# A feed-forward block split in two stages: seven half-size products for gate and up, with the gated values kept in DRAM

## The chip, the cores and the metric

The kernel runs on one core of a Trainium2 chip. The metric is the device time in microseconds of one execution. The core has a matrix engine (PE, with a weight-load side called PEld), a vector engine (DVE), a scalar engine (ACT), GpSimd (POOL) and a sync engine (SP) whose queue issues most DMAs. The profile gives times from the start of its span.

## The reference, cut to what matters

One layer: a mixing block (an RG-LRU next to RWKV-7 heads), its output projection, a gated feed-forward network, a gated embedding, and a last norm. There are S = 512 tokens, D = 2048 features and D_FF = 6144. The change touches the feed-forward part:

```
h = h + concat(out_a, out_b) @ w_o
u = rmsnorm(h, ln_ffn)
gate = causal_dwconv(u @ w_gate, conv_f_w, conv_f_b)      # 3 taps over tokens
h = h + (gelu(gate) * (u @ w_up)) @ w_down
u = rmsnorm(h, ln_ple)                                    # then the gated embedding
```

All is float32. Every matrix product is made of three: each operand is split into a high part hi (rounded to fp32r) and the rest lo, and hi x hi, hi x lo and lo x hi are added in PSUM.

## The kernel before, in words

Values are held with features on partitions: a tile hT[m] is 128 features by 512 tokens. `wqueue` gets the list of all weight tiles in the order of use. `wfill` (L105) keeps two of them ahead of the product that is at work: it loads a raw tile of 128x1024 (SP queue, two buffers), ACT copies it to hi (L127), DVE subtracts to get lo (L128); hi and lo have three buffers each. An entry of the list can be a function that makes the raw tile itself (loads, sums). `wfill` runs with a raised priority. In this phase no order is written out by hand: instructions go to the queues of the engines by priority, which is the order of the program with such offsets, and each queue is worked off in order.

`phase2` begins with the second part of the output projection (16 row tiles; L1188 adds to hT, L143/L144 split it as the operand u of the next products, POOL sums squares).

The FFN runs in one interleaved order, `ffn_order`. For each of 48 feature tiles f of D_FF and for gate and up there are two units of 8 k-tiles: 24 matmuls of 128x128 weights against 512 tokens (L1216 to L1218). L1238 to L1244 scale the gate by the token norm, apply the convolution and the gelu, and multiply by the norm once more (POOL); L1249 multiplies by up. Four tiles f make a chunk of 512 hidden features, kept in SBUF; `hidden` forms its operands.

The down product of a chunk uses a seven-product scheme (Winograd's form of Strassen's method) on halves of hidden features, tokens and output columns: 7 products of half size for 8. `down_unit` makes the sums of weight blocks; one block is added to another in SBUF by a DMA from the POOL queue that accumulates (L1127). Each product has 12 matmuls of 512 columns (L1298 to L1300), and DVE adds it out of PSUM to the running sums (L1313). The 14 down units of a chunk are spread between the gate/up units of the next. The last chunk is done plainly (`down_last`), followed for each block of 512 output columns by `to_features` (transposes and splits for the next stage). The residual hT is transposed to tokens-on-partitions early, in `turn`, during the first chunk.

After that come the gated embedding (L1389 to L1391; the last quarter is 256 columns wide) and the final norm.

Of the kernel before, what the change touches and what calls it, by code (L numbers as in the profile page):

```python
# [4 lines left out]
F32 = mybir.dt.float32  # L5
# [6 lines left out]
D = 2048  # L12
# [9 lines left out]
FC = 4  # L22
C = 64
# [62 lines left out]
class Builder:  # L86
# [149 lines left out]
    def xsplit(self, k):  # L236
        return (self.t(self.bp, "xh%d" % k, (128, S), F32R, bufs=1),
                self.t(self.bp, "xl%d" % k, (128, S), F32R, bufs=1))
# [827 lines left out]
    def wo_a(self, m):  # L1066
        nc, A, k1 = self.nc, self.A, self.k1
        if m == 0:
            self.out_a(range(4, 8))
            self.hT = [self.bp.tile([128, S], F32, tag="x%s%d" % ("hl"[i // 8], 8 + i % 8), name="hT%d" % i, bufs=1)  # L1070
                       for i in range(KT)]
# [29 lines left out]
    def ffn_order(self):  # L1101
        g = lambda f: [("g", f, w, h) for w in range(2) for h in range(2)]
        o = sum([g(f) for f in range(FC)], [])
        nch = NF // FC
        for ch in range(nch - 1):
            q = [("q", ch, b, i) for b in range(2) for i in range(7)]
            o += g((ch + 1) * FC)
            n = sum([g((ch + 1) * FC + i) for i in range(1, FC)], [])
            k = 0
            for i, x in enumerate(q):  # L1110
                o.append(x)
                e = (i + 1) * len(n) // len(q)
                o += n[k:e]
                k = e
        o += [("d", cb, kh) for cb in range(4) for kh in range(2)]
        return o


    def down_unit(self, ch, b, i):
        nc = self.nc  # L1120

        def load(kh, nh):
            t = self.t(self.k2, "hw%d" % (2 * kh + nh), (128, 2, 512), bufs=1)
            nc.sync.dma_start(t, self.A["wd"][ch, b, kh, nh])
            return t
        def add(t, kh, nh):
            nc.gpsimd.dma_start(t, self.A["wd"][ch, b, kh, nh], accum_op=ALU.add)  # L1127

        def sum_of(kh, nh):
            t = self.t(self.k2, "hw4" if nh == 0 else "hw1", (128, 2, 512), bufs=1)  # L1130
            nc.sync.dma_start(t, self.A["wd"][ch, b, kh, nh])
            return t
        if i == 0:
            self.qt = sum_of(0, 0)
            add(self.qt, 0, 1)
            return load(0, 0)
        if i == 1:
            self.qs = sum_of(0, 1)
            add(self.qs, 1, 1)
            return self.qt  # L1140
        if i == 2:
            add(self.qt, 1, 1)
            return self.qt
        if i == 3:
            return load(1, 1)
        if i == 4:
            return self.qs
        if i == 5:
            return load(1, 0)
        add(self.qt, 1, 0)  # L1150
        return self.qt

    def ffn_items(self):
        A = self.A
        u = (128, 8, 128)
        r = []
        for o in self.ffn_order():
            if o[0] == "g":
                r.append((A["wgu"][o[1], o[2], o[3]], u))
            elif o[0] == "d":  # L1160
                r.append((A["wd"][NF // FC - 1, o[1] % 2, o[2], o[1] // 2], (128, 2, 512)))
            else:
                r.append((lambda o=o: self.down_unit(*o[1:]), (128, 2, 512)))
        for cb in range(4):
            r += [(A["wpp"][cb], (128, 2, 512))]
            if cb < 3:
                r += [(A["wpg"][cb, i], (128, 2, 512)) for i in range(8)]
        r += [(A["wpg3"][0, i], (128, 4, 256)) for i in range(2)]
        r += [(A["wpg3"][1, 0, :, 2 * i:2 * i + 2], (128, 2, 256), "hw%d" % (4 + i)) for i in range(2)]
        r += [(A["wpg3"][0, i], (128, 4, 256)) for i in range(2, 4)]  # L1170
        r += [(A["wpg3"][1, i], (128, 4, 256)) for i in range(1, 4)]
        return r


    def phase2(self):
# [8 lines left out]
        u2 = []  # L1184
        for m in range(KT):
# [3 lines left out]
            hi, lo = T("uh%d" % m, dt=F32R), T("ul%d" % m, dt=F32R)  # L1189
            self.split(hi, lo, hT[m], self.P("ln_ffn", m))  # L1190
            u2.append((hi, lo))
            if m == 0:
                SC.activation(acc, hT[m], AF.Square)
            else:
                sq = T("tmp", 2)
# [3 lines left out]
        gz = self.t(self.cp, "row", (128, S + 2), bufs=1)  # L1199
        G.memset(gz[:, 0:2], 0.0)  # L1200


        h3 = [self.bp.tile([128, S], F32, tag="x%s%d" % ("hl"[i // 8], i % 8), name="h3_%d" % i, bufs=1) for i in range(16)]

        def turn(cb):
            for tt in range(4):
                pt = self.mm()
                for i in range(4):
                    TE.transpose(pt[:, i * 128:(i + 1) * 128], hT[4 * cb + i][:, tt * 128:(tt + 1) * 128], self.K("ident"))
                SC.activation(h3[tt * 4 + cb], pt, AF.Copy)  # L1210

        def half(ps, us, h):
            wh, wl = self.wnext()
            for k in range(8):
                xh, xl = us[8 * h + k]
                TE.matmul(ps, wh[:, k, :], xh, start=h + k == 0, stop=False)  # L1216
                TE.matmul(ps, wh[:, k, :], xl, start=False, stop=False)  # L1217
                TE.matmul(ps, wl[:, k, :], xh, start=False, stop=h == 1 and k == 7)  # L1218

        raw = [None, None]  # L1220
        pgu = [None, None]
        gc = None

        def gate_up(f, which, h):
            nonlocal gc
            if h == 0:
                pgu[which] = self.aux() if f >= FC else self.mm()
            half(pgu[which], u2, h)
            if h == 0:
                return  # L1230
            if which == 0:
                if f == 0:
                    self.r2 = self.tok_rstd(acc, D, RMS_EPS, k2)
                    return
            elif f == 0:
                self.rstd_bcast(acc, D, RMS_EPS, k2, rs, self.r2)
            if which == 0 or f == 0:
                V.tensor_tensor(gz[:, 2:S + 2], pgu[0], rs, ALU.mult)  # L1238
                gc = c = T("tmp", 2)
                SC.activation(c, gz[:, 2:S + 2], AF.Identity, scale=self.P("cfw", 2 * NF + f), bias=self.P("cfb", f))  # L1240
                for w in range(2):
                    V.scalar_tensor_tensor(c, gz[:, w:w + S], self.P("cfw", w * NF + f), c, ALU.mult, ALU.add)
                SC.activation(c, c, AF.Gelu_apprx_tanh)  # L1243
                G.tensor_tensor(c, c, rs, ALU.mult)  # L1244
            if which == 1:
                i = f % FC
                if i % 2 == 0:
                    raw[i // 2] = T("hw%d" % (5 + i // 2), 1, (128, 2, 512))
                V.tensor_tensor(raw[i // 2][:, i % 2, :], gc, pgu[1], ALU.mult)  # L1249
                if i < 4:  # L1250
                    turn(i) if f < FC else None
                if i == FC - 1:
                    self.hids[f // FC] = hidden(f == NF - 1)


        a = lambda i, j: raw[j][:, :, 256 * i:256 * i + 256]

        def hidden(last):
# [335 lines left out]
```

## Time and profile before

| | us |
|---|---|
| median of 3 runs | 2648.77 (2645.67 to 2649.02) |
| the profiled execution | 2648.61 |
| its span | 2646.8 |

| stretch of the span, us | what runs there |
|---|---|
| 0 to 908 | mixing block and output projection |
| 908 to 1026 | gate and up of the first chunk |
| 1026 to 2377 | gate and up with the down products of 11 chunks |
| 2380 to 2437 | last chunk, turn to features |
| 2437 to 2647 | gated embedding, final norm |

In the page, "busy" is a sum of instruction lengths. Matmuls overlap, so that a busy PE is not yet a PE at its peak; the distance from one start to the next tells more. In a row of groups, the number after the bar is the busy time, then the mean length in ns, then the engine's idle time before these instructions and what ended it.

### The profile page before, as it was taken

Reading aid. Unit: us, or ns where it says so; the run is one execution under the profiler, and the core shown is the slowest. Engines: PE = TensorE matmul, PEld = TensorE weight load, DVE = VectorE, ACT = ScalarE, POOL = GpSimd, SP = SyncE. Lnnn points to the kernel's source line nnn. Section 1 sums busy time; section 2 is a strip of 40 time slices with the busy share of each in tenths; the row PEclk is TensorE's granted clock in tenths of the full one; section 3 lists DMA queues with packets and bytes.
Section 4 is the critical chain, followed back from the end, with each engine's and each line's share of the span. In section 5 each row is a group of like instructions: output and inputs, shape, how many; then the busy total and the mean of one; then the engine's idle time right before and its main releaser. Section 6 shows DMA issues by size and latency. Waiting matters only on the chain.

```text
span 2646.8 us, 43808 instructions
## 1 busy us (share of the span) xinstructions
PE 2602.5 (98%) x18466; PEld 2132.7 (81%) x18466; DVE 1614.5 (61%) x2332; ACT 1081.6 (41%) x1515; POOL 278.9 (11%) x265
## 2 busy tenths in 40 slices
PE   9989999999999999999999999999999999999997
PEld 8867778777877888888888888888888888888887
DVE  5764775667666535565665665666566565775447
ACT  6563555546433433333333333333333333335335
POOL 0010000101122301101011110101010111000001
PEclk9999999999999999999999999999999999999999
DMA  7222322222234324545455454545454545442223
GB/s 251 90 69 66 93 77 63 84 75 94 95 128 138 117 88 120 153 133 152 134 151 137 143 138 141 153 133 152 137 156 129 153 139 152 131 137 88 96 92 108
DMA packets 100326, 323.26 MB, mean 122 GB/s; under 512 B 11552, under 2 KB 14240, under 8 KB 100128
## 3 DMA queue, kind: packets, MB, share of 16 engines
q1 hardware_dynamic: 87456, 274.32, 30.7%
q0 software_dynamic: 12672, 46.14, 10.5%
q8 instruction: 144, 2.36, 0.4%
q14 instruction: 54, 0.44, 0.1%
HBM read 312.29 MB, written 8.13 MB: 121 GB/s over the span
## 4 chain that ended last, share of the span: by engine, by line
PE 69%; DVE 2%; DMA 1%; ACT 1%; issue 1%; POOL 0%; POOLq 0%; ACTq 0%; DVEq 0%
PE wk L1218 12%; PE wk L1217 12%; PE wk L1216 12%; PE mm L1299 6%; PE mm L1300 6%; PE mm L1298 6%; PE mm L1389 2%; PE mm L1391 2%; PE mm L1390 2%; PE mm L161 1%; PE mm L157 1%; PE mm L159 1%; PE mm L1216 1%; PE mm L1218 1%; PE mm L1217 1%
## 5 line engine op out<-in xcount | busy, mean ns | idle before, releaser
L127 ACT ACTIVATE whi<-wraw 128x1024 fp32r<-128x1024 f32 (+1 forms) x361 | 373.8, 1035 | 736.9 <-PE mm L159 194.2
L128 DVE TENSOR_TENSOR wlo<-wraw,whi 128x1024 fp32r<-128x1024 f32 (+1 forms) x361 | 441.7, 1223 | 241.5 <-ACT whi L127 235.6
L1216 PE MATMUL wk<-uh,whi 128*128 128x512 f32 x1408 | 547.9, 389 | 0.0
L1218 PE MATMUL wk<-uh,wlo 128*128 128x512 f32 x1408 | 547.8, 389 | 0.0
L1217 PE MATMUL wk<-ul,whi 128*128 128x512 f32 x1408 | 547.8, 389 | 0.0
L127 ACT ACTIVATE whi<-hw 128x1024 fp32r<-128x1024 f32 x154 | 163.4, 1061 | 488.7 <-PE wk L1217 389.9
L128 DVE TENSOR_TENSOR wlo<-hw,whi 128x1024 fp32r<-128x1024 f32 x154 | 188.7, 1226 | 243.7 <-ACT whi L127 241.3
L161 PE MATMUL mm<-xh,wlo 128*128 128x512 f32 x832 | 333.2, 400 | 1.5 <-DVE wlo L128 1.5
L157 PE MATMUL mm<-xh,whi 128*128 128x512 f32 x832 | 333.1, 400 | 1.4 <-DVE hT L447 0.9
L159 PE MATMUL mm<-xl,whi 128*128 128x512 f32 x832 | 331.8, 399 | 0.0
L1216 PEld LDWEIGHTS wk<-uh,whi 128*128 128x128 f32 x1408 | 264.3, 188 | 54.9
L1217 PEld LDWEIGHTS wk<-ul,whi 128*128 128x128 f32 x1408 | 264.3, 188 | 54.9
L1218 PEld LDWEIGHTS wk<-uh,wlo 128*128 128x128 f32 x1408 | 264.3, 188 | 54.8
L1299 PE MATMUL mm<-wlo,hid 128*128 128x512 f32 x680 | 265.2, 390 | 0.0
L1300 PE MATMUL mm<-whi,hid 128*128 128x512 f32 x680 | 264.9, 390 | 0.0
L1298 PE MATMUL mm<-whi,hid 128*128 128x512 f32 x680 | 264.9, 390 | 0.0
L157 PEld LDWEIGHTS mm<-xh,whi 128*128 128x128 f32 x832 | 157.5, 189 | 37.6 <-issue 3.0
L161 PEld LDWEIGHTS mm<-xh,wlo 128*128 128x128 f32 x832 | 157.5, 189 | 36.6 <-DVE wlo L128 2.6
L159 PEld LDWEIGHTS mm<-xl,whi 128*128 128x128 f32 x832 | 157.4, 189 | 33.7 <-issue 1.8
L1313 DVE TENSOR_TENSOR h<-h,mm 128x512 f32<-128x512 f32 x264 | 175.2, 682 | 0.9
L1244 POOL TENSOR_TENSOR tmp<-tmp,rsa 128x512 f32<-128x512 f32 x48 | 70.3, 1464 | 772.1 <-ACT tmp L1243 772.1
L1298 PEld LDWEIGHTS mm<-whi,hid 128*128 128x128 f32 x680 | 127.7, 188 | 26.4
(511 smaller groups left out, 3550.3 us busy)
## 6 DMA issues: line engine op xcount, KB each, us to landing
wraw<-wgu SPq DMA_DIRECT2D x192, 512.0 KB, 3.3
hw<-wd SPq DMA_DIRECT2D x110, 512.0 KB, 3.2
hw<-wd POOLq DMA_DIRECT2D x88, 512.0 KB, 5.5
wraw<-wz SPq DMA_DIRECT2D x80, 512.0 KB, 3.6
wraw<-wpg SPq DMA_DIRECT2D x31, 512.0 KB, 3.2
wraw<-wo SPq DMA_DIRECT2D x22, 512.0 KB, 3.8
wraw<-wo SPq DMA_DIRECT2D x20, 256.0 KB, 2.9
tmp<-xT SPq DMA_DIRECT2D x16, 256.0 KB, 2.7
```

What stands on the lines that cost most here:

```text
L127: nc.scalar.activation(hi, raw, AF.Copy)
L128: nc.vector.tensor_tensor(lo, raw, hi.bitcast(F32), ALU.subtract)
L157: nc.tensor.matmul(ps, hi[:, k, :], xh, start=first and i == 0, stop=False)
L159: nc.tensor.matmul(ps, hi[:, k, :], xl, start=False, stop=False)
L161: nc.tensor.matmul(ps, lo[:, k, :], xh, start=False, stop=last and i == n - 1)
L1216: TE.matmul(ps, wh[:, k, :], xh, start=h + k == 0, stop=False)
L1217: TE.matmul(ps, wh[:, k, :], xl, start=False, stop=False)
L1218: TE.matmul(ps, wl[:, k, :], xh, start=False, stop=h == 1 and k == 7)
L1298: TE.matmul(ps, x[0][:, k, ts_], w[0][:, k, :], start=first and k == 0, stop=False)
L1299: TE.matmul(ps, x[0][:, k, ts_], w[1][:, k, :], start=False, stop=False)
L1300: TE.matmul(ps, x[1][:, k, ts_], w[0][:, k, :], start=False, stop=last and k == 1)
L1313: V.tensor_tensor(o, o, ps[tt], op)
```

## The change

The FFN is cut in two stages. The first makes all gate/up products and writes the gated values to DRAM; the second loads them as operands of the down products.

**Gate and up.** The seven-product scheme now serves these as well, on halves of the input features (1024), of a pair of feature tiles (2 x 128) and of the tokens (2 x 256). For each of 24 pairs p and w = gate, up there are seven products (q5, p1, p4, p6, p7, p2, p3), each one unit of 24 matmuls with 256 columns. Their token operands are built once, in `forms`, during the output projection; their weight operands are made by `gate_unit`: plain loads (p1, p2, p4), sums on DVE (q5, p7), and accumulating DMAs from POOL's queue (p6, p3). `gate_up` combines the results with DVE. The token norm is applied to the gate alone; the factor for up is applied at the end of the block, where the sum is per token (`rt`).

**Gated values.** `spill` writes a chunk's four tiles to DRAM (rd), and four differences of their quarters (dd). `hidden` loads a quarter or a difference and splits it.

**Down.** Chunks go in groups of 3, 3, 3 and 2 which accumulate in PSUM; the seven sums are kept apart (PT) and combined once at the end. `down_unit` makes two of the weight sums on DVE and two by accumulating DMAs. While the second half of a group (b = 1) runs, the operands of the next group are loaded. The residual waits in DRAM (hd) and is transposed at the end, in `residual`.

Tiles hi and lo of one operand now share one buffer (`xsplit`). The core of the diff:

```
+GROUPS = [(0, 3), (3, 6), (6, 9), (9, 11)]
+KORDER = [(0, 1, 4, 5, 2, 3, 6, 7), range(8)]
...
+    def gate_order(self, p, w):
+        return ("p1", "p4", "p2", "q5", "p7", "p6", "p3") if p + w == 0 else ("q5", "p1", "p4", "p6", "p7", "p2", "p3")
+    def gate_unit(self, p, w, u):
+        nc, par = self.nc, 4 * (w % 2)
+        src = lambda i, j: self.A["wgu"][2 * p + i, w, j]
+        buf = lambda n: self.t(self.bp, "x%d" % (par + n), (128, 8, 128), bufs=1)
...
+        if u == "q5":
+            self.g21, self.g22, self.gs = load(0, 1, 0), load(1, 1, 1), buf(3)
+            nc.vector.tensor_tensor(self.gs, self.g21, self.g22, ALU.add)
+            return self.gs
...
+        if u == "p7":
+            if first:
+                self.g11 = load(2, 0, 0)
+            nc.vector.tensor_tensor(self.g21, self.g21, self.g11, ALU.add)
+            return self.g21
+        nc.gpsimd.dma_start(self.gs, src(0, 0 if u == "p6" else 1), accum_op=ALU.add)
+        return self.gs
...
+        if i == 1:
+            self.d1[c], self.dq[c] = load(buf(21 + c), 0, 1), buf(24 + c)
+            nc.vector.tensor_tensor(self.dq[c], self.d0[c], self.d1[c], ALU.add)
+            return self.dq[c]
...
+        nc.gpsimd.dma_start(self.dq[c], src(1, 1 if i == 2 else 0), accum_op=ALU.add)
+        return self.dq[c]
...
+        def part(ps, u):
+            wh, wl = self.wnext()
+            for k in range(8):
+                xh, xl = X[u][k // 2][:, k % 2, 0], X[u][k // 2][:, k % 2, 1]
+                TE.matmul(ps, wh[:, k, :], xh, start=k == 0, stop=False)
+                TE.matmul(ps, wh[:, k, :], xl, start=False, stop=False)
+                TE.matmul(ps, wl[:, k, :], xh, start=False, stop=k == 7)
...
+                if u == "p1":
+                    SC.activation(fm[:, 0], at, AF.Copy)
+                if u == "p6":
+                    V.tensor_tensor(v, at, fm[:, 0], ALU.subtract)
+                    V.scalar_tensor_tensor(fm[:, 1], low[:, 256:512], -1.0, v, ALU.mult, ALU.subtract)
+                if u in ("p6", "p7") and {"p6", "p7"} <= done:
+                    V.tensor_tensor(x, v, bank["p7"], ALU.subtract)
+                    V.tensor_tensor(two(out[:, 1]), two(low), x.unsqueeze(1).broadcast_to([128, 2, 256]), ALU.add)
+                if u == "p3":
+                    V.tensor_tensor(two(out[:, 0]), two(up), fm[:, 0:2], ALU.add)
...
+        def spill(ch, raw):
+            a = lambda i, j: raw[j][:, :, 256 * i:256 * i + 256]
+            for j in range(2):
+                nc.sync.dma_start(rd[ch][j], raw[j])
...
+        for p in range(NF // 2):
+            z, c = B(8), B(9)
+            gate_up(p, 0, z)
+            conv(p, z, c)
+            r = B(10 + p % 3)
+            gate_up(p, 1, r)
+            V.tensor_tensor(r, r, c, ALU.mult)
...
+        def down(g, b):
+            lo, hi = GROUPS[g]
+            for i in range(7):
+                ps = [self.mm(), self.mm()]
+                for ch in range(lo, hi):
+                    w = self.wnext()
+                    for tt in range(2):
+                        product(ps[tt], hids[ch, i], w, tt, ch == lo, ch == hi - 1)
                 for tt in range(2):
+                    o = PT[i][b][:, tt]
+                    if g == 0:
                         SC.activation(o, ps[tt], AF.Copy)
                     else:
+                        V.tensor_tensor(o, o, ps[tt], ALU.add)
+                if b == 1 and g + 1 < len(GROUPS):
+                    group_form(g + 1, i)
...
+        for cb in (0, 2, 1, 3):
+            residual(cb)
+            down_last(cb)
+            to_features(cb)
```

More of the change, by code (lines that the diff above doesn't have):

```diff
@@ L1198, in phase2 @@
         rs = self.rsa
[L1199 to L1210, printed above, removed]
@@ new lines, in hidden, with quarter, group_form @@
+        def hidden(src, tag):
+            r = T("tmp", 3, (128, 2, 256))
+            nc.sync.dma_start(r, src)
+            t = T("s%d" % tag, 1, (128, 2, 2, 256), F32R)
+            self.split(t[:, 0], t[:, 1], r)
+            return t[:, 0], t[:, 1]
+        def quarter(ch, i, j):
+            return rd[ch][j][:, :, 256 * i:256 * i + 256]
+        hids = {}
+        def group_form(g, i):
+            lo, hi = GROUPS[g]
+            for ch in range(lo, hi):
+                src = {0: quarter(ch, 0, 0), 5: quarter(ch, 0, 1), 6: quarter(ch, 1, 1)}.get(i)
+                if src is None:
+                    src = dd[ch][(i - 1) // 2][:, (i - 1) % 2]
+                hids[ch, i] = hidden(src, 3 * i + ch - lo)
```

362 lines of the change are left out of this document (183 added, 179 removed).

## The prediction

> **What bounds the kernel now.** I read the profile page first, then the groups by line with shapes kept apart, then single matmuls on the timeline, and last the windows, the DMAs and the waits of the weight path. The page and the groups say whose time it is:
>
> ```profile
> span 2646.8 us, 43808 instructions
> ...
> PE 2602.5 (98%) x18466; PEld 2132.7 (81%) x18466; DVE 1614.5 (61%) x2332; ACT 1081.6 (41%) x1515; POOL 278.9 (11%) x265
> ```
> ```profile
> L1216 PE MATMUL wk<-uh,whi 128*128 128x512 f32 x1408 | 547.9, 389 | 0.0
> L1218 PE MATMUL wk<-uh,wlo 128*128 128x512 f32 x1408 | 547.8, 389 | 0.0
> L1217 PE MATMUL wk<-ul,whi 128*128 128x512 f32 x1408 | 547.8, 389 | 0.0
> ...
> L1300 PE MATMUL mm<-whi,hid 128*128 128x512 f32 x680 | 264.9, 390 | 0.0
> ...
> L1216 PE MATMUL mm<-uh,whi 128*128 128x512 f32 x128 | 50.2, 392 | 0.0
> ```
>
> The reader sees PE at 98%, and zero idle time ahead of the gate/up matmuls (L1216 to L1218) and of the down matmuls (L1298 to L1300). There are (1408 + 128) x 3 = 4608 gate/up matmuls and 3 x 680 = 2040 down matmuls. The 389 ns of a row is a length with overlap; what counts is the distance from start to start. One for each width:
>
> ```profile
> 1500.29 0.39 PE L1216 MATMUL wk<-uh,whi 128*128 128x512 f32 x1
> ...
> 1502.33 0.39 PE L1216 MATMUL wk<-uh,whi 128*128 128x512 f32 x1
> ```
> ```profile
> 2585.10 0.28 PE L1390 MATMUL mm<-wlo,uh 128*128 128x256 f32 x1
> ...
> 2587.98 0.28 PE L1390 MATMUL mm<-wlo,uh 128*128 128x256 f32 x1
> ```
>
> Nine 512-column matmuls take 2.04 us, 0.2267 each. Twenty-four 256-column ones take 2.88 us, 0.120 each, each with its own 128x128 weight load as in the changed kernel. So half the columns cost 53% of the time. The gate/up products hold 4608 x 0.2267 = 1044.6 us of the span and nothing waits in them. A unit is one weight tile of 128x1024: 24 matmuls, 5.44 us of PE, and one split (ACT writes hi, DVE writes lo).
>
> **The matmuls (the gain).** Seven products of half size replace eight. After: 24 pairs of features x 2 (gate, up) x 7 products x 8 k x 3 = 8064 matmuls of 256 columns, 8064 x 0.120 = 967.7 us. The change of PE work is 967.7 - 1044.6 = **-76.9 us**. The down products keep their 2040 matmuls, and the 64 transposes of the residual only move from the first chunk to the end: zero on PE. The spacing at which the gain is gone is 1044.6 / 8064 = 0.1295 us.
>
> The rule that I weigh here is in the Trainium skill, "TensorE: Matmul & The Clock Gate", section "Back-to-back issue gap": a warm matmul alone takes N/2.4 + 2.5 ns, 215.8 at 512 and 109.2 at 256. By it the gate/up stage would go from 994.4 to 880.6 us, a gain of 113.8. The rows of this trace show a larger fixed part, 226.7 against 2 x 120 ns, and the measurement decides.
>
> **What has to hide under PE now.** A gate/up unit shrinks from 5.44 to 24 x 0.120 = 2.88 us, but its split stays as it was, and there are 336 units where there were 192. The durations:
>
> ```profile
> L128 DVE TENSOR_TENSOR wlo<-wraw,whi 128x1024 fp32r<-128x1024 f32 x341 | 425.8, 1249 | 237.3 <-ACT whi L127 231.6 <-PE wk L199 4.2 <-PE mm L161 0.7
> L127 ACT ACTIVATE whi<-wraw 128x1024 fp32r<-128x1024 f32 x341 | 361.2, 1059 | 691.7 <-PE wk L1217 162.0 <-PE mm L159 160.7 <-PE mm L1300 129.3
> ...
> L1313 DVE TENSOR_TENSOR h<-h,mm 128x512 f32<-128x512 f32 x264 | 175.2, 682 | 0.9
> ...
> L1242 DVE SCALAR_TENSOR_TENSOR tmp<-row,par,tmp 128x512 f32<-128x512 f32 x96 | 71.7, 747 | 1.5 <-ACT tmp L1240 1.0
> ...
> L1240 ACT ACTIVATE tmp<-row,par 128x512 f32<-128x512 f32 x48 | 39.1, 815 | 0.0
> ```
> ```profile
> L1409 DVE TENSOR_TENSOR e<-e,hw x16: 424/686/693, 2479.3 to 2615.5; 128x512 f32<-128x512 f32 x12, 128x256 f32<-128x256 f32 x4
> ```
>
> Take a step of one feature pair and one of gate or up: 7 units, 20.16 us of PE. DVE then has 7 lo splits x 1.249 = 8.74; two sums of weight tiles of 128x1024 (no such row; the lo split of the same size is the nearest) = 2.50; three 256-wide combinations x 0.424 = 1.27; two 512-wide ones x 0.682 = 1.36; half of a pair's two 1024-wide multiplies = 1.25; half of its four convolution steps x 0.747 = 1.49; a quarter of a chunk's four differences for DRAM x 0.68 = 0.68. Sum 17.3 us of 20.16, 86%. ACT has 7 x 1.059 and less than 2 us beside. DVE stays under PE by 2.9 us a step, so the stage stays PE's; what DVE could cost is a split that comes late.
>
> How late it may come: there are three buffers for a split, so ACT may start a unit's split when PE ends the third unit before it, two units ahead of need: 10.88 us before, 5.76 after. How long it takes:
>
> ```profile
> 1504.64 0.69 DVE L1249 TENSOR_TENSOR hw<-tmp,wk 128x512 f32<-128x512 f32 x1 [3.14 <-PE wk L1218]
> 1505.36 0.69 DVE L1276 TENSOR_TENSOR hid<-hw,hw 128x512 f32<-128x512 f32 x1
> 1505.97 1.22 DVE L128 TENSOR_TENSOR wlo<-wraw,whi 128x1024 fp32r<-128x1024 f32 x1
> ```
> ```profile
> 1504.34 1.06 ACT L127 ACTIVATE whi<-wraw 128x1024 fp32r<-128x1024 f32 x1 [4.10 <-PE wk L1217]
> ```
>
> From ACT's start at 1504.34 to the end of lo at 1507.19 it is 2.85 us, with two other DVE operations ahead of it; without them it is 1.06 + 1.25 = 2.3. So 2.9 to 3.5 us are left for DVE's other work, four or five operations of 0.7 us. I price late splits in the gate/up stage at 2 us (bounds 0 and 30; near 0, since even a dense run of DVE work cost half a microsecond here).
>
> **The accumulating DMAs.** Two of seven products (p6, p3) take a tile onto which a POOL DMA adds a further weight block, after the lo split of an earlier product: 96 in this stage, and 44 in the down stage where there were 88.
>
> ```profile
> L1127 POOL DMA_DIRECT2D hw<-wd x88: 852/874/1072, 846.1 to 2337.2; - x88
> ...
> DMA to landing us min/median/max: 5.1/5.5/8.6
> ```
>
> In the order q5, p1, p4, p6, p7, p2, p3 each waits for a product three units ahead. That split is done 2 x 2.88 - 2.3 = 3.5 us ahead of its own unit; the next must start 3 x 2.88 - 2.3 = 6.3 us after that unit's start. So 9.8 us are free for a landing of 5.5, or 8.6 at the worst: no stall. POOL has little else there: its 48 multiplies of L1244 go away. The DMA load rises:
>
> ```profile
> q1 hardware_dynamic: 87456, 274.32, 30.7%
> q0 software_dynamic: 12672, 46.14, 10.5%
> ```
> ```profile
> core 0: us, PE busy (x) PEld busy (x) DVE busy (x) ACT busy (x) POOL busy (x), PEclk, DMA share, GB/s
> ...
> 2000.00:2125.00 125.00, 125.00 (x554) 103.49 (x553) 75.89 (x94) 41.22 (x46) 12.87 (x12) 1.00 0.52 143
> ```
>
> 30.7% of 2646.8 us for 274.32 MB is 2.96 us a MB, so 1.55 us for a 0.524 MB load; 10.5% for 46.14 MB is 3.16 us for an accumulation. A step has 4 loads, 2 accumulations and one spill on average: 5 x 1.55 + 2 x 3.16 = 14.1 us of 20.16, a share of 0.70 where the window shows 0.52. Longer landings, but with 4.3 us of slack at the median. The spills and the later re-reading (46 writes of 512 KB, 81 loads of 256 KB) stand in SP's queue among the weight loads; a spill that waits for DVE holds those behind it, but the buffer of a gate weight is free some ten units, 29 us, before the weight is needed. Cost 0.
>
> **The start of the stage.**
>
> ```profile
> wraw<-wgu SPq DMA_DIRECT2D x192, 512.0 KB, 3.3
> ```
>
> Tiles x0 to x7 hold operands of the output projection until its last matmul, so the first q5 sum comes late; the first step therefore runs p1, p4, p2 first and has q5, p7, p6, p3 behind each other. There p6 is only two units behind q5, and p3 next to p6. From the end of the projection: two loads 4 (the row says 3.3 for one), sum 1.3, split 2.3, accumulation 5.5, split 2.3 make 15.4 us against 5 x 2.88 = 14.4 for p6, then 7.8 us more against 2.88 for p3. Stall 1 + 4.9 = 5.9 us. DVE also builds the operands there:
>
> ```profile
> 840.00:908.00 68.00, 66.33 (x289) 53.70 (x289) 40.17 (x47) 31.56 (x46) 24.80 (x16) 1.00 0.53 166
> ```
> ```profile
> L144 DVE SCALAR_TENSOR_TENSOR ul<-hT,par,uh 128x512 fp32r<-128x512 f32 x16 | 14.0, 875 | 0.8 <-ACT uh L143 0.8
> ```
>
> Of the 16 tiles, the first eight now take three 256-wide operations for one of 0.875 (+0.4 each), the other eight nine (+2.9): 27 us on top of these 40 of 68. Full, but their last ones are needed 5 us into the stage. Together **+7 us** (bounds 0, if PE is given other work, and 15).
>
> **The down stage.** Now by itself: 154 units of 12 matmuls, 2.72 us each. DVE a unit: 1.249, 2/7 of a sum 0.36, and a third of two PSUM additions 0.45 (three chunks now accumulate in PSUM, so 84 additions replace L1313's hundreds): 2.06. In the second half of each group it also splits the next group's operands, 0.69 a unit: 2.75 of 2.72. So DVE is full half the time, but those splits have some 50 us until they are needed. The accumulations run three in a row 2.72 us apart, with 5 x 2.72 - 4.6 = 9.0 us free for the landing; in the last group of two chunks 4 x 2.72 - 4.6 = 6.3. **+5 us** (0 to 20). The end trades 20 DVE additions for 14 larger ones and adds 16 that read the residual back: +1 (0 to 4).
>
> **Sum.** -76.9 + 2 + 7 + 5 + 1 = -61.9. The profiled execution took 2648.6 us (span 2646.8 and 1.8 around it), the median of the runs is 2648.8: **2587 us**.
>
> **Rivals.**
> A. DVE couples in more than this: at 86 to 100% its queue, kept in order, holds splits back behind convolution steps that wait for ACT. At 0.7 us in every step of 7 units and half a microsecond in a third of the down units that is 48 x 0.7 + 51 x 0.5 = 59 us in place of 7: 2639 us. For it: margin per unit falls from 8 to 3 us. Against: the run of DVE operations above cost no matmul anything.
> B. Slower: the accumulation becomes the bound of every step. Place: p6 and p3. It decides from a landing above 9.8 us; the net 61.9 us over 96 accumulations is 0.64, so from 10.4 us the gain is gone, and at 11.5 the stage loses 163 us: 2750 us. For it: DMA share 0.70, descriptors by POOL. Against: the largest of 88 was 8.6.
> C. The spacing of matmuls is another. These rows have a shorter one, with another tile as the moving operand:
>
> ```profile
> 2608.49 0.28 PE L1390 MATMUL mm<-hw,uh 128*128 128x256 f32 x1
> ...
> 2608.95 0.28 PE L1391 MATMUL mm<-hw,ul 128*128 128x256 f32 x1
> ```
> Four in 0.46 us, 0.115: 927.4 us, 2547 in all. Or a weight load that isn't hidden sets the pace. If the exposed part were 16 ns, 0.136 a matmul makes 1096.7 us: 2716. The first rule above lies near the short end (0.109). The same section of the Trainium skill also states for sustained streams about 131 ns a matmul at N=512 and 81 at N=128; drawn straight between these, an estimate of 98 ns at 256 would make the change a loss, 604 to 790 us, but the rows' 226.7 ns contradict its first figure.
> D. No change in matmul count is not possible, as the loops are fixed; gain and stalls could cancel within 0.2%, about what a measurement of this kernel can tell from no change.
>
> **Chances.** Forecast (stalls under 40 us) 0.72; A 0.13, of which 0.02 ends at no difference and 0.01 slower; B 0.07; C short 0.05, C long 0.02; D 0.01. Faster 0.72 + 0.10 + 0.05 = 0.87, the same 0.03, slower 0.01 + 0.07 + 0.02 = 0.10. The range runs from 2560 (no stalls is 2572; a part of C) to 2630 (most of A); outside are B, C's ends and the worst of A, some 0.17.
>
> **What would show it.** Right: gate/up matmuls 0.120 us apart, 8064 of them; PE idle under 1% from the second step to the end of the down stage; DVE near 85% in the gate/up windows; accumulation landings below 9.8 us; one gap of several microseconds in the first step. Wrong: matmuls that wait for lo splits or whi in every step (A), splits that wait for accumulations (B), a spacing other than 0.120 (C).

## The result: 2720.4 us, slower, and the profile after

| | us |
|---|---|
| before, median of 4 runs | 2648.03 (2645.67 to 2649.02) |
| after, median of 4 runs | 2720.41 (2718.62 to 2723.74) |
| ratio after to before | 1.0276, 95% interval 1.0258 to 1.0294 |
| after, the profiled execution | 2718.62, span 2716.5 |

Predicted were 2587 us and a gain. First the page of the changed kernel: the span, the busy times and the DMA queues (packets, MB, share of 16 engines).

```profile
span 2716.5 us, 51689 instructions
...
PE 2584.5 (95%) x21922; PEld 2257.1 (83%) x21922; DVE 1901.9 (70%) x2594; ACT 1241.8 (46%) x1743; POOL 254.6 (9%) x268
...
q1 hardware_dynamic: 111056, 317.58, 33.6%
q0 software_dynamic: 20160, 73.41, 16.2%
```

PE is busy for 18 us less than before, in a span that is 70 us longer: it now waits, which it did little before. Is it the matmuls? On the timeline, two rows 24 gate/up matmuls apart:

```profile
1507.88 0.28 PE L1264 MATMUL mm<-s,whi 128*128 128x256 f32 x1
...
1510.76 0.28 PE L1264 MATMUL mm<-s,whi 128*128 128x256 f32 x1
```

That is 2.88 us, 0.120 for each, just as in the last quarter of the embedding before. So the waits are what is new. PE's longest, from its table of waits (total, times, longest):

```profile
PE mm L1266 <- DVE wlo L131: 35.2, 51, 3.0
PE mm L1370 <- DVE wlo L131: 20.1, 25, 2.4
PE mm L1369 <- ACT whi L130: 19.5, 17, 3.2
PE mm L1264 <- ACT whi L130: 9.2, 13, 2.9
```

The gate/up matmuls (L1264 to L1266) and the down matmuls (L1369 to L1371) wait for splits of weights. The lo split of DVE, by which most of them are released, is not the cause yet; what held that split must be found.

From the starts of all matmuls the sum can be made anew. A gate/up unit needs 2.88 us, a down unit 12 x 0.2267 = 2.72; what a unit takes beyond that is counted as stall.

| term | predicted | measured |
|---|---|---|
| matmuls of gate and up | -76.9 | -76.9 (8064 at 0.120 us) |
| first step (start of the stage) | +7 | +20.9 |
| the other 47 steps (late splits) | +2 | +56.9 |
| down stage | +5 | +65.4 |
| end, and what is left over | +1 | +3.4 |
| sum | -61.9 | +69.7 (2716.5 - 2646.8) |

The gain came in full, and three stalls took 143 us.

**The 47 steps.** The accumulating DMA of the gate/up stage, and the table of who waits for it, in the changed kernel:

```profile
L1132 POOL DMA_DIRECT2D x<-wgu x96: 862/875/1085, 923.0 to 1941.4; - x96
...
ACT whi L130: 254.2, 60
...
DMA to landing us min/median/max: 5.1/5.5/9.2
```

At the median it lands in 5.5 us, as predicted. But the first and the last of 96 stand 1018.4 us apart; there are two in a step, 8.3 us apart, so one round takes (1018.4 - 8.3) / 47 = 21.5 us. PE needs 20.16. One round on the timeline (start, length, engine, idle time before and what ended it):

```profile
1506.21 0.89 POOL L1132 DMA_DIRECT2D x<-wgu  x1 [14.40 <-DVE wlo L131]
1514.38 0.87 POOL L1132 DMA_DIRECT2D x<-wgu  x1 [7.28 <-DVE wlo L131]
1526.45 0.88 POOL L1132 DMA_DIRECT2D x<-wgu  x1 [11.19 <-DVE wlo L131]
...
1511.66 2.01 ACT L130 ACTIVATE whi<-x 128x1024 fp32r<-128x1024 f32 x2 [0.70 <-PE mm L1266]
...
1519.86 2.01 ACT L130 ACTIVATE whi<-x 128x1024 fp32r<-128x1024 f32 x2 [3.12 <-DMA x<-wgu]
...
1520.95 1.22 DVE L131 TENSOR_TENSOR wlo<-x,whi 128x1024 fp32r<-128x1024 f32 x1 [2.16 <-ACT whi L130]
1522.21 1.23 DVE L1120 TENSOR_TENSOR x<-x,x 128x1024 f32<-128x1024 f32 x1
1523.36 0.41 DVE L1292 TENSOR_TENSOR x<-x,wk 128x256 f32<-128x256 f32 x1
1523.69 1.22 DVE L1130 TENSOR_TENSOR x<-x,x 128x1024 f32<-128x1024 f32 x1
1524.82 1.22 DVE L131 TENSOR_TENSOR wlo<-x,whi 128x1024 fp32r<-128x1024 f32 x1
```

Follow it. At 1506.21 POOL issues p6's block. It lands 5.34 us later, at 1511.55, and at 1511.66 ACT splits p6 (the row names PE, which set a buffer free at about the same time; over the stage ACT starts p6 0.1 us after the landing in 46 of 47 steps). DVE follows, and as soon as lo is done POOL issues p3's block (1514.38): 8.17 us. It lands at 1519.86, and ACT, which takes its work in the order of the list, splits p3 and right behind it the next step's q5. DVE makes lo of p3 at 1520.95; then its queue holds two sums of weights (L1120, L1130) and a combination, so that lo of q5 starts at 1524.82, some 3 us after its hi was done. Then the next p6 is issued, 1526.45. The round is 20.24 us here, against 20.16: **a loop of two accumulations, three splits and two sums, which closes on itself once in a step**. It has nothing to give: a longer landing shows at once. In the round above both blocks land in 5.4 us; in the next one p3's takes 8.3, and that round is 23.07 us long. The median hides such landings: p3's take 5.6 us on average in the steps for up, but 7.4 in the steps for gate, which no run here explains. The two landings of a round come to 11.9 us on average. Over the stage, lo of q5 ends 0.7 us after its own unit has begun (median), not 3.5 us ahead of it.

**The down stage.** Its accumulations, with POOL's idle time by releaser, and three in a row, behind the split that the second of them (2177.62) follows and the two of ACT that start at landings:

```profile
L1158 POOL DMA_DIRECT2D s<-wd x44: 862/875/888, 1964.4 to 2417.1; - x44
...
issue: 99.5, 17
...
DMA to landing us min/median/max: 5.3/6.0/9.2
```
```profile
2166.53 1.22 DVE L131 TENSOR_TENSOR wlo<-s,whi 128x1024 fp32r<-128x1024 f32 x1
...
2168.90 1.06 ACT L130 ACTIVATE whi<-s 128x1024 fp32r<-128x1024 f32 x1 [2.83 <-DMA s<-wd]
...
2177.41 1.06 ACT L130 ACTIVATE whi<-s 128x1024 fp32r<-128x1024 f32 x1 [6.93 <-DMA s<-wd]
...
2169.11 0.87 POOL L1158 DMA_DIRECT2D s<-wd  x1 [5.36 <-DVE s L144]
2177.62 0.89 POOL L1158 DMA_DIRECT2D s<-wd  x1 [7.64 <-issue]
2183.31 0.88 POOL L1158 DMA_DIRECT2D s<-wd  x1 [4.80 <-issue]
```

No two are closer than 5.62 us. POOL waits 99.5 us for "issue", that is for nothing that the profile shows: the split that the accumulation of 2177.62 has to follow was done at 2167.75. What ends the wait shows in the landings. One block lands, ACT starts its split 0.1 us later (2168.90, 2177.41), and POOL issues the next one 0.2 us after that (2169.11, 2177.62). So it is with 36 of the 43 that have one ahead of them, whatever releaser their rows name; the other seven come after a pause. There are never two under way. 50 of the 65 us lie in the units of the third product, whose weight tiles (three, in the last group two) each take an accumulation: by group and half 7.6, 6.9, 6.3, 7.5, 6.4, 6.0, 4.8 and 4.2.

**The first step.** Windows of the changed kernel (busy PE, PEld, DVE, ACT, POOL, then clock, DMA share, GB/s), and rows of the projection's second half:

```profile
840.00:908.00 68.00, 67.13 (x297) 55.30 (x296) 64.41 (x107) 44.30 (x87) 18.72 (x12) 1.00 0.46 151
...
908.00:922.00 14.00, 9.19 (x59) 8.54 (x58) 14.00 (x23) 9.36 (x18) 3.67 (x2) 0.85 0.90 335
...
1000.00:1900.00 900.00, 862.13 (x7034) 847.87 (x7034) 672.34 (x755) 360.66 (x396) 72.83 (x83) 1.00 0.62 173
```
```profile
902.74 0.47 DVE L147 SCALAR_TENSOR_TENSOR s<-hT,par,s 128x256 fp32r<-128x256 f32 x1
903.14 0.41 DVE L144 TENSOR_TENSOR s<-tmp,s 128x256 fp32r<-128x256 f32 x1
903.47 1.52 DVE L147 SCALAR_TENSOR_TENSOR s<-hT,par,s 128x256 fp32r<-128x256 f32 x1
...
896.77 1.84 POOL L1251 TENSOR_TENSOR acc<-acc,tmp 128x512 f32<-128x512 f32 x1 [4.26 <-ACT tmp L1250]
902.87 1.84 POOL L1251 TENSOR_TENSOR acc<-acc,tmp 128x512 f32<-128x512 f32 x1 [4.26 <-ACT tmp L1250]
```

DVE needs 6.10 us a tile of the projection (902.87 - 896.77) where PE needs 5.44, falls behind, and is busy without a gap in the first 14 us of the stage. In every tile the same operation (L147) takes once 0.47 and once 1.52 us, the latter while POOL adds the squares (L1251). The two operations ahead of it, at 902.74 and 903.14, keep their lengths although POOL's addition has begun by its record; that addition takes 1.84 us, where the shortest takes 1.3.

### The profile page after: what moved, and what is told of

Same layout as the page of the kernel before. It is cut to its first block, busy times and chain, and to the rows that moved or that the text cites. A ratio compares the mean times of both kernels' runs of the same rounds, so it can differ in the third digit from the quotient of the medians.

```text
span 2716.5 us, 51689 instructions
## 1 busy us (share of the span) xinstructions
PE 2584.5 (95%) x21922; PEld 2257.1 (83%) x21922; DVE 1901.9 (70%) x2594; ACT 1241.8 (46%) x1743; POOL 254.6 (9%) x268
## 4 chain that ended last, share of the span: by engine, by line
issue 21%; PE 19%; DMA 17%; DVE 11%; ACT 3%; POOL 2%; POOLq 0%; ACTq 0%; DVEq 0%; SPq 0%
DMA x<-wgu 16%; DVE wlo L131 5%; ACT whi L130 2%; PE mm L1266 2%; PE mm L1475 2%; PE mm L1477 2%; PE mm L1476 2%; PE mm L1264 2%; PE mm L1265 2%; POOL s L1158 1%; PE mm L1370 1%; PE mm L1371 1%; PE mm L1369 1%; PE wk L1264 1%; PE wk L1265 1%
## 5 line engine op out<-in xcount | busy, mean ns | idle before, releaser
L1266 PE MATMUL mm<-s,wlo 128*128 128x256 f32 x1920 | 552.7, 288 | 35.8 <-DVE wlo L131 35.2
L130 ACT ACTIVATE whi<-x 128x1024 fp32r<-128x1024 f32 x330 | 337.3, 1053 | 528.9 <-DMA x<-wgu 254.2
L1264 PE MATMUL mm<-s,whi 128*128 128x256 f32 x1920 | 548.1, 285 | 11.0 <-ACT whi L130 9.2
L131 DVE TENSOR_TENSOR wlo<-x,whi 128x1024 fp32r<-128x1024 f32 x330 | 401.7, 1221 | 210.0 <-ACT whi L130 209.2
L1265 PE MATMUL mm<-s,whi 128*128 128x256 f32 x1920 | 546.0, 284 | 0.2 <-DVE s L144 0.2
L1266 PEld LDWEIGHTS mm<-s,wlo 128*128 128x128 f32 x1920 | 370.5, 193 | 48.1 <-DVE wlo L131 47.9
L1264 PEld LDWEIGHTS mm<-s,whi 128*128 128x128 f32 x1920 | 370.8, 193 | 14.3 <-ACT whi L130 12.2
L1265 PEld LDWEIGHTS mm<-s,whi 128*128 128x128 f32 x1920 | 370.7, 193 | 0.5 <-DVE s L144 0.4
L160 PE MATMUL mm<-x,whi 128*128 128x512 f32 x832 | 333.1, 400 | 0.9 <-DVE hT L450 0.9
L164 PE MATMUL mm<-x,wlo 128*128 128x512 f32 x832 | 332.8, 400 | 0.0
L162 PE MATMUL mm<-x,whi 128*128 128x512 f32 x832 | 331.2, 398 | 0.0
L1369 PE MATMUL mm<-whi,s 128*128 128x512 f32 x680 | 272.7, 401 | 19.6 <-ACT whi L130 19.5
L1371 PE MATMUL mm<-whi,s 128*128 128x512 f32 x680 | 270.7, 398 | 0.0
L1266 PE MATMUL wk<-s,wlo 128*128 128x256 f32 x768 | 218.2, 284 | 0.8 <-DVE wlo L131 0.8
L1264 PE MATMUL wk<-s,whi 128*128 128x256 f32 x768 | 218.1, 284 | 0.0
L1265 PE MATMUL wk<-s,whi 128*128 128x256 f32 x768 | 217.9, 284 | 0.0
```

Of the source, the lines that this page charges most:

```text
L130: nc.scalar.activation(hi, raw, AF.Copy)
L131: nc.vector.tensor_tensor(lo, raw, hi.bitcast(F32), ALU.subtract)
L160: nc.tensor.matmul(ps, hi[:, k, :], xh, start=first and i == 0, stop=False)
L162: nc.tensor.matmul(ps, hi[:, k, :], xl, start=False, stop=False)
L164: nc.tensor.matmul(ps, lo[:, k, :], xh, start=False, stop=last and i == n - 1)
L1264: TE.matmul(ps, wh[:, k, :], xh, start=k == 0, stop=False)
```

## The experiments

Three theories, one for each stall: the 47 steps are held by the loop above; the down stage by the descriptors of POOL's accumulations, if the program's memory for them holds those of only one DMA; the start by DVE, slowed by POOL. The main rival for the first and the last is that DVE is simply too full (the prediction's rival A), for the second that the DMAs themselves are what is slow. Each run is one execution, but for the one with all three edits. "Before" took 2642 us beside the first four, 2647 beside the next, 2648 beside the last two. All stalls in one table, worked out as above:

| run | us | first step | 47 steps | down stage |
|---|---|---|---|---|
| changed kernel | 2718.6 | 20.9 | 56.9 | 65.4 |
| descriptors 2048 bytes | 2679.5 | 20.9 | 59.6 | 25.8 |
| other weights for p6, p3 | 2652.2 | 22.0 | 0.0 | 63.3 |
| sums on POOL | 2785.5 | 26.3 | 117.0 | 65.8 |
| part of the forms on POOL | 2735.6 | 26.1 | 61.5 | 71.6 |
| order of the sums | 2662.9 | 19.9 | 0.7 | 66.6 |
| order, 2048 bytes | 2617.9 | 20.4 | 0.0 | 24.4 |
| square sum on DVE | 2703.5 | 12.4 | 54.9 | 65.8 |
| order, 2048 bytes, square sum | 2609.8 | 11.9 | 0.9 | 25.1 |
| only the other buffer | 2727.8 | 21.7 | 63.6 | 70.0 |
| descriptors 1024 bytes | 2678.8 | 22.9 | 57.5 | 26.6 |

**More memory for descriptors.** The larger memory needs room, so the square sum takes a buffer that is free then.

```
-        acc = T("acc")
+        acc = self.rsa
-    nc = _bacc.Bacc("TRN2", target_bir_lowering=False, num_devices=1, dynamic_dma_scratch_size=512)
+    nc = _bacc.Bacc("TRN2", target_bir_lowering=False, num_devices=1, dynamic_dma_scratch_size=2048)
```

> The descriptor memory for POOL's DMAs grows from 512 to 2048 bytes; the square sums move into a tile that is free (2 KB make room). In the trace after, accumulating DMAs follow each other by no less than 5.6 us, and the down stage loses 51 of its 65 us of stalls in product i=2, where three accumulations in a row are wanted 2.7 us apart. Theory 1 (accumulations cannot overlap because the descriptor ring holds one): spacing falls to about 3 us, stalls at i=2 from 51 to under 12 us, total near 2680; the gate/up stage, where they are 8 us apart anyway, stays within 5 us of 1045. Theory 2 (the DMA engines are too loaded in the down stage, 0.7 of their time): spacing and total stay within 5 us of 2718.

Measured: 2679.54 us. Accumulations now follow each other as DVE's splits allow, down to 1.73 us apart:

```profile
2149.88 0.86 POOL L1158 DMA_DIRECT2D s<-wd  x1 [2.77 <-DVE wlo L131]
2151.61 0.86 POOL L1158 DMA_DIRECT2D s<-wd  x1 [0.87 <-DVE wlo L131]
```

The wait for "issue" is gone from POOL's table, and the third product's stalls fell from 50 to 14.5 us (the 51 of the expectation has two units of the product before in it), although the median landing grew from 6.0 to 7.0. The gate/up stage did not change: there the accumulations are 8 us apart anyway.

**Other weights for p6 and p3.** All DMAs, sums and splits stay; only no product waits for an accumulation.

```
         nc.gpsimd.dma_start(self.gs, src(0, 0 if u == "p6" else 1), accum_op=ALU.add)
-        return self.gs
+        return self.g22
```

> Products p6 and p3 of the gate/up stage split a tile that is already there (the plain block of p4) in place of the tile that the accumulating DMA makes; all DMAs, sums and splits are still issued, so the weights of p6 and p3 are other ones. Theory 1 (a loop: lo of q5, accumulation, split of p6, accumulation, split of p3, and behind it in ACT's order the next q5; some 20 to 21 us round against 20.2 of matmuls): without the landings the stalls of the steady steps fall from 57 to under 12 us, first step too by some 6; the total is near 2665. Theory 2 (DVE, 77% busy, is simply too full and its queue holds splits back): q5 keeps its 29 us of stalls, and the total stays above 2690.

Measured: 2652.16 us. The 47 steps have no stall left; nearly every round is 20.16 us, PE's own time. The window of this run, to be held against the changed kernel's row from 1000 to 1900:

```profile
1500.00:1600.00 100.00, 100.00 (x836) 100.00 (x835) 81.21 (x91) 45.70 (x49) 8.80 (x10) 1.00 0.67 178
```

DVE does the same work in less time, busy for 81% instead of 75, and holds up nobody. So it is not DVE's load.

**The two sums on POOL.** If two sums in DVE's queue lengthen the loop, they could go to an engine that has time.

```
-            nc.vector.tensor_tensor(self.gs, self.g21, self.g22, ALU.add)
+            nc.gpsimd.tensor_tensor(self.gs, self.g21, self.g22, ALU.add)
...
-            nc.vector.tensor_tensor(self.g21, self.g21, self.g11, ALU.add)
+            nc.gpsimd.tensor_tensor(self.g21, self.g21, self.g11, ALU.add)
```

> The two sums of weight tiles of a gate/up step go from DVE to POOL. In the trace after, lo of q5 stands behind both in DVE's order and starts 2.9 us after hi is there. Theory 1 (loop): 2.5 us less in the round, so it falls under the time of the matmuls: steady stalls from 57 to under 20 us, total near 2680. Theory 2 (DVE's load): 96 x 2 x 1.13 us / 2 of DVE time less, stalls fall to a similar value, so this run tells the two apart only together with the one without landings. Rival 3: POOL's additions are slow (3 us each) and hold POOL's queue, or block DVE; then the accumulations come later still and the total rises over 2720.

Measured: 2785.46 us, the mean round 22.8. On the timeline:

```profile
1498.53 3.26 POOL L1130 TENSOR_TENSOR x<-x,x 128x1024 f32<-128x1024 f32 x1
...
1499.46 3.42 DVE L131 TENSOR_TENSOR wlo<-x,whi 128x1024 fp32r<-128x1024 f32 x1
...
1504.66 1.22 DVE L131 TENSOR_TENSOR wlo<-x,whi 128x1024 fp32r<-128x1024 f32 x1
```

While POOL's addition runs, DVE's subtraction does not get on: it ends at 1502.88, 1.09 us after POOL's addition, and takes 3.42 us where it takes 1.22 alone. The page "SBUF — State Buffer" of the Trainium skill, section "SBUF: two separate sides", describes that: a VectorE operation with two inputs from SBUF and a GpSimd operation that reads SBUF share a pair of ports, held for the whole instruction. These rows agree. The sums left DVE's queue and still stood in the way of its splits.

**Part of the forms on POOL**, to relieve DVE in the start (the difference of two quarters and the operand of p7, for the second eight tiles).

```
-            V.tensor_tensor(d, h12, h11, ALU.subtract)
+            (V if k == m else G).tensor_tensor(d, h12, h11, ALU.subtract)
...
-            SC.activation(f1[:, 1], halves(hT[k])[1], AF.Copy, scale=g0)
+            SC.activation(f1[:, 1], halves(hT[k])[0], AF.Copy, scale=g0)
...
-            V.scalar_tensor_tensor(f3[:, 0], b, g, f1[:, 1], ALU.mult, ALU.subtract)
+            G.tensor_tensor(f3[:, 0], f2[:, 0], f1[:, 1], ALU.subtract)
```

> While the operands are built, two of the 256-wide DVE operations of each of the last eight feature tiles go to POOL (the difference of token halves and the p7 operand, by another formula of the same value). In the trace after, DVE turns round in 6.1 us a tile where the matmuls need 5.44, and the first gate/up step stalls by 15 us on operands and lo splits and by 6 on accumulations. If DVE's load there is the cause: a tile takes 5.4 to 5.5 us, and the first step loses under 10 us in place of 21; total 2705 to 2710. If the stall comes from the order of splits and not from the load: less than 4 us of change.

Measured: 2735.63 us; a miss. The period of a tile grew from 6.1 to 6.8 us, since other operations now meet POOL's:

```profile
889.46 1.65 POOL L1233 TENSOR_TENSOR tmp<-tmp,tmp 128x256 f32<-128x256 f32 x1 [1.94 <-DVE tmp L1231]
...
890.44 0.96 DVE L1232 SCALAR_TENSOR_TENSOR tmp<-hT,par,tmp 128x256 f32<-128x256 f32 x1
```

L1232 takes 0.47 us in the changed kernel. What is taken off DVE is paid back by what waits.

**The order of the two sums in DVE's queue.** The sums need not stand where they stand: L1120's is for the q5 of the step after, L1130's for p7, four units behind q5. Nothing else changes. (In this run and those built on it, numbers of lines are one to three higher.)

```
-            nc.vector.tensor_tensor(self.gs, self.g21, self.g22, ALU.add)
+            with self.tc.issue_after(self.los[-3].ins):
+                nc.vector.tensor_tensor(self.gs, self.g21, self.g22, ALU.add)
...
-            nc.vector.tensor_tensor(self.g21, self.g21, self.g11, ALU.add)
+            with self.tc.issue_after(self.los[-2].ins):
+                nc.vector.tensor_tensor(self.g21, self.g21, self.g11, ALU.add)
```

> Edit: only the order of VectorE's queue in the gate/up stage is changed: the sum of the next q5 stands behind the lo split of the entry three before it in the list, the sum of p7 behind the lo split of the entry two before it, so that no sum stands between the hi and the lo split of q5. Theory 1 (a loop of hi, lo, accumulation, hi, lo, accumulation, hi closes once in a step, and two weight sums in VectorE's queue make it 20.3 us against 20.16 us of TensorE): the loop falls by about two sums, to some 17.8 us, the steady stalls of the stage from 57 to under 15 us, the whole from 2719 to about 2672 us. Rival (VectorE is simply too full, 77% of the stage, and its work only changes places): steady stalls stay above 45 us, the whole at 2705 to 2725 us. Rival 2 (the landing of the accumulations sets the round whatever stands in VectorE's queue): no change either.

Measured: 2662.90 us, and 0.7 us of stalls in 47 steps; more than expected, since the loop now has time in hand and takes up single long landings (up to 9.7 us). Issues on POOL, and DVE between p3's landing and q5's lo:

```profile
1513.09 0.88 POOL L1135 DMA_DIRECT2D x<-wgu  x1 [12.29 <-DVE wlo L132]
1521.05 0.87 POOL L1135 DMA_DIRECT2D x<-wgu  x1 [7.09 <-DVE wlo L132]
1531.60 0.88 POOL L1135 DMA_DIRECT2D x<-wgu  x1 [9.67 <-DVE wlo L132]
...
1527.77 1.22 DVE L132 TENSOR_TENSOR wlo<-x,whi 128x1024 fp32r<-128x1024 f32 x1 [0.94 <-ACT whi L131]
1528.92 0.41 DVE L1295 TENSOR_TENSOR x<-x,wk 128x256 f32<-128x256 f32 x1
1529.36 0.69 DVE L1296 TENSOR_TENSOR x<-mm,x 128x512 f32<-128x512 f32 x1
1529.97 1.22 DVE L132 TENSOR_TENSOR wlo<-x,whi 128x1024 fp32r<-128x1024 f32 x1
```

No sum stands between the two lo splits any more; this round is 18.5 us. The landings, the load of DVE and the count of everything are as they were: the loop through DVE's order was the cause, and the too full DVE is out.

**Order and 2048 bytes together.** Both diffs as above.

> Edit: the order of the two weight sums as in the run before, and 2048 bytes in place of 512 for the descriptors of GpSimd's DMAs (the square sum takes another buffer to make room). If the two causes are separate, their gains add: -41 (down stage) and -47 (gate/up stage) from 2719 give about 2631 us, below the kernel before. If the gate/up loop also hung on the descriptor memory, or if the denser down stage fills the DMA engines, the sum falls short: 2650 us or more.

Measured: 2617.93 us. The causes are separate: 57 and 41 us go, each where it did alone; the sum expected counted 10 us too few for the first.

**The square sum on DVE.**

```
-                G.tensor_tensor(acc, acc, sq, ALU.add)
+                V.tensor_tensor(acc, acc, sq, ALU.add)
```

> Edit: the sum of squares of the output projection's tiles is added on VectorE, no longer on GpSimd; nothing else. Theory (a GpSimd addition shuts VectorE's two-input operations out while it runs, 1.52 us for one that takes 0.47 otherwise): the tile period of the second half of the projection falls from 6.09 to about 5.6 us although VectorE has one operation more, the stall of the first step from 21 to about 15 us, the whole by some 6 us to about 2713. Rival (VectorE is merely full there): with one operation more the period grows to 6.5 us, and the whole to about 2723.

Measured: 2703.50 us. DVE has one operation more in each tile, and the period fell to 5.66 us (from one L1251 to the next), with no operation of 1.52 us in it:

```profile
889.24 0.69 DVE L1251 TENSOR_TENSOR acc<-acc,tmp 128x512 f32<-128x512 f32 x1
...
890.18 0.88 DVE L147 SCALAR_TENSOR_TENSOR s<-hT,par,s 128x256 fp32r<-128x256 f32 x2
...
894.90 0.70 DVE L1251 TENSOR_TENSOR acc<-acc,tmp 128x512 f32<-128x512 f32 x1
```

The first step lost 8.5 us of its stall. With the other two edits in place it does the same, from 20.4 to 11.9 us. The other 7 us of the gain lie ahead of the stage, which begins at 901.5 instead of 908.1; among the runs with the same code up to there it begins between 900.1 and 908.3, so nothing is concluded from them.

**All three**, run four times.

> Edit: all three together: the order of the two weight sums, 2048 bytes for the descriptors, the square sum on VectorE. If the three causes are separate and are those found: 2719 - 41 - 47 - 6 = about 2625 us, a ratio to the kernel before of 0.991, faster than both. What would then be left of the predicted 2587 are the first step's stall (15), the down stage (25) and the end. If they are not separate: 2645 or more.

Measured: 2609.75 us median (2608.84 to 2614.75), ratio to the kernel before 0.9867, 95% interval 0.9847 to 0.9886: 1.3% less time, clear of the scatter, but less than the 2% from which a kernel is called faster here. Against the change as it was made, measured at another time, it is 4.1% less. From its page:

```profile
PE 2542.1 (98%) x21922; PEld 2240.4 (86%) x21922; DVE 1903.1 (73%) x2609; ACT 1254.1 (48%) x1743; POOL 228.4 (9%) x253
```

PE is at 98% again, with DVE's work the same. What is left of the stalls is 12 us in the first step, where 7 were predicted, and 25 in the down stage, where 5 were, 12 of these in its first half group.

**Only the other buffer**, since the run with 2048 bytes had changed two things at once.

```
-        acc = T("acc")
+        acc = self.rsa
```

> Edit: the square sum takes another buffer, as in the run with 2048 bytes, but the descriptors of GpSimd's DMAs keep their 512 bytes. Theory (the descriptor memory alone gave the 41 us): no change, 2714 to 2724 us, accumulations of the down stage 5.6 us apart at the least. Rival (the other buffer gave it): about 2680 us.

Measured: 2727.78 us, accumulations at least 5.60 us apart, POOL's wait for "issue" 102.5 us. The buffer gives nothing. The time is 4 us above the range that was expected; the down stage lost 5 us more and the 47 steps 7 us more than in the profile of the changed kernel, and why is open.

**1024 bytes**, with the other buffer. With 1024 bytes alone the tiles no longer fit: a partition has 120.66 KB left where they need 120.84.

> Edit: the square sum's other buffer and 1024 bytes for the descriptors of GpSimd's DMAs. Theory (512 bytes hold the descriptors of one 512 KB accumulation, so that the next is not issued before the first has landed): 1024 bytes hold two, the least distance falls to 1.7 to 3 us for pairs, the third of a row still waits for the first; of the down stage's 65 us of stalls some 28 to 38 stay, the whole at 2681 to 2692 us, a little behind the 2679.5 of 2048 bytes. Rival (any other reason for the 5.6 us): no change, 2714 to 2724 us.

Measured: 2678.81 us, distances down to 1.73 us, 26.6 us of stalls in the down stage: the same as with 2048. The rival is out: the memory for descriptors sets the distance. But 1024 bytes do not hold just two: here as with 2048 the trace has up to three under way at once (issued at 1962.14, 1965.55 and 1967.82, the first of them landing at 1969.68), so a third does not wait. How many bytes one accumulation takes, and when they come free, stays open.

## Why the prediction was wrong

- **Matmuls**: right, in count (8064), spacing (0.120) and gain. By the rule of the Trainium skill weighed there ("TensorE: Matmul & The Clock Gate", section "Back-to-back issue gap") a unit would take 2.62 us; it takes 2.88.
- **Late splits in the gate/up stage**, +2 with a bound of 30, became 57. The step that failed is "That split is done 2 x 2.88 - 2.3 = 3.5 us ahead of its own unit", from which followed "So 9.8 us are free for a landing of 5.5". It took for q5 that ACT starts when the buffer comes free and that DVE follows at once. Of the 2.3 us it became 6.5 from the buffer to the end of lo (median): 1.4 until ACT is through with p3, then some 3 us behind two sums. And p3 is late because p6 was, which hung on q5 before it. Each accumulation was priced by itself, from a split assumed on time; the chain that goes through both of them and back to q5 wasn't added up. The prediction's own numbers show such a round to be over the bound: two landings of 5.5, three splits of 2.3 and two sums, 2.5, are 20.4 us, against 20.16. That alone would make 11 us in 47 steps. Most of the rest goes with the landings: with the 11.9 us that two of them took on average the same sum is 21.3, and 21.5 were measured.
- **Rival B** had the right place, p6 and p3, and the wrong condition ("It decides from a landing above 9.8 us"). The median landing stayed at 5.5, the longest was 9.2, and B's bound was there all the same. **Rival A** named DVE's queue in order, rightly, but as a matter of load. DVE was at 75% of the stage in the changed kernel (86% predicted), and at 80% without the stalls; the order of two operations was worth 56 us.
- **The down stage**, +5 with a bound of 20, became 65. The step that failed is "The accumulations run three in a row 2.72 us apart, with 5 x 2.72 - 4.6 = 9.0 us free for the landing". They could not run 2.72 us apart. The trace of before had no row against it, since its accumulations were never closer than 8.28 us; the bounds should have held the case in which they don't overlap: at 5.5 instead of 2.72 us the third of a row is issued 2 x 2.8 = 5.6 us late in six half groups, and the second of two 2.8 us late in the last two, up to 39 us if nothing hides it. In the units of these rows 50 were measured.
- **The start**, +7 with a bound of 15, became 21. The step that failed is "27 us on top of these 40 of 68. Full, but their last ones are needed 5 us into the stage". It spread the work over both halves of the projection, though nearly all of it falls on the last eight tiles: before, DVE was busy for 25.6 of the 44 us from 864 to 908, 3.2 us a tile, and the prediction's own +2.9 makes that more than the 5.44 us that PE needs. And it took operations at their lengths when alone: of the 6.10 us measured a tile, 1.05 are the one operation that takes 1.52 us instead of 0.47 beside POOL's addition. That part is shown (8.5 us); the 12 us that then remain weren't taken apart, and the granted clock of 0.85 in the stage's first 14 us wasn't priced either.
- **DMA**: the predicted share of 0.70 is that of the stage without its stalls (0.69 from 1000 to 1800 us with the sums in order; 0.62 with the stalls).
- **The end**, +1 (0 to 4), was about 3.

Open: the remaining 25 us of the down stage, of which 12 in its first half group, where the operands from DRAM and the first accumulations meet; no run here separates them.

## What to carry to other kernels

When a step's products depend on each other through a transfer, price the whole round, from one product by every queue and transfer back to the same product of the next step, and hold it against the time of a step; slack that is counted for each transfer alone counts the same microseconds again and again. Price the transfers of such a round at their mean and not at their median, since in a closed round every long one counts. In an engine worked off in order, ask what stands ahead of the one operation that a loop goes through: a busy share says nothing about that. And before you let several transfers of one kind overlap, look for two that do so in the trace; if there are none, price them one after the other.

## What the runs showed of the hardware

- With 512 bytes for the descriptors of POOL's DMAs, accumulations of 512 KB were never less than 5.6 us apart, and never two under way: in a row each was issued 0.3 us after the landing of the one before, without a wait for that in the program. With 1024 or 2048 bytes up to three were under way, down to 1.73 us apart. In the profile this wait has no name but "issue", or that of another engine.
- Accumulations that overlap land later: median 6.0 us one at a time, 7.0 to 7.3 together in the down stage.
- POOL's additions and DVE's operations with two inputs hold each other up: a subtraction of 128x1024 went from 1.22 to 3.42 us, one of 128x256 from 0.47 to 0.96 or 1.5; POOL's own addition of 128x512 took 1.3 to 1.84 us.
- A change in which every wait is short can lose more than it gains: 51 waits of L1266, 0.7 us on average, are 35 of the gate/up stage's 78 us.
